# Modulation vectors of the first sub-layer: eight fp32 matmuls in one run, a small fold matmul, and a later place for the second scale and the squares

## The chip, the core and the metric

The kernel runs on one core of a Trainium2 chip. The metric is the time of one execution on the device in microseconds (us); less is better. Five engines work side by side, each through its own list of instructions: TensorE (PE in the profile, PEld for its weight loads), VectorE (DVE), ScalarE (ACT), GpSimd (POOL) and SyncE (SP), which here issues nearly all transfers.

## The reference

Two layers over 512 latent tokens and 256 context tokens, width 1024. Each sub-layer normalizes its input, scales and shifts it by vectors that come from the conditioning, and adds a gated result. Cut to what matters here:

```python
silu_c = jax.nn.silu(c)
silu_cc = jax.nn.silu(c_ctx)
for i in range(DEPTH):
    m_lat = (silu_c @ ada_w[i] + ada_b[i]).reshape(b, N_SUBLAYERS, N_MOD, 1, d)
    m_ctx = (silu_cc @ ada_w[i] + ada_b[i]).reshape(N_SUBLAYERS, N_MOD, 1, d)
    h = norm_modulate(x_lat, norm_g[i, 0], m_lat[:, 0, 0], m_lat[:, 0, 1])   # rms_norm(x, g) * (1 + scale) + shift
    x_lat = x_lat + MACARON_WEIGHT * m_lat[:, 0, 2] * swiglu(h, ffn_w_in[i, 0], ffn_w_out[i, 0])
    ...
```

The first sub-layer (a SwiGLU feed-forward) needs three such vectors of 1024 numbers, shift, scale and gate, each for the latent and for the context conditioning. They are the subject of the change.

## The kernel before

Everything is kept with features on the 128 partitions and tokens along the free dimension. A product in nearly full fp32 precision is made of three fp32r matmuls (`mm3`, L882 to L885): high part of the weights by high part of the data, high by low, low by high. ScalarE makes a high part by a copy (L206), VectorE the low part by a subtraction (L207). Input products of a feed-forward are done by Strassen-like products of half-size blocks; the first three output chunks of the first sub-layer go straight instead, so that they can begin before the norm is known.

Those straight products are twelve numbered steps. Steps 0 to 2 are the chunks 0 to 2 with the first half of K and the first 384 tokens ("00"), steps 3 to 5 the same chunks with the second half of K ("01"), steps 6 to 8 and 9 to 11 the same for the second 384 tokens. A step has four rounds k of six matmuls (gate and up weights, three each), 24 in all; step 0 uses the tile tB11 (the scaled input, high and low), step 3 tB21, step 6 tB12. The table `hooks` (L1804 to L1821) says what else is written behind round k of step n: the entry (3, 1) is emitted behind round 1 of step 3. While these steps last, TensorE, SyncE, ScalarE and VectorE all run in the written order, so the table fixes what stands ahead of what in each queue.

A modulation vector is computed as two half vectors hm of 512 numbers: hm 2 and 3 are the scale, 0 and 1 the shift, 4 and 5 the gate. In the hooks they are called scale0, scale1, shift0, shift1, gate0 and gate1. One half vector goes through `ada_direct` (L496) in stages, each `run(..., 1)` doing one:

1. Four fp32 matmuls (L501), k = 0 to 3. Each has 128 x 32 weights (`silu_p`, of whose 32 columns two are used) and 512 columns of `ada_w`, and goes to its own 32 columns of TensorE's array and its own 32 partitions of one PSUM bank.
2. Four more, k = 4 to 7, that add to the same places.
3. ScalarE copies the bank to SBUF (`adr`, L507).
4. Four transposes by TensorE (L511) of 128 x 128 each, VectorE's sum over the four groups (`ads`, L513), and VectorE's addition of the bias into `mods` (L484).

The second scale half also needs `scale_vec` (L669, the tile `scl`); then "early" (L800 to L808) makes tB21 of the input and that scale, ScalarE the high and VectorE the low part. "fill" splits the weights of a following step (w or lateG tiles). "squares" has ScalarE square an input chunk (L628) and VectorE add it to `ssq` (L633); "parts" splits the sum (th by ScalarE, L652; tl by VectorE, L653); "root" has TensorE add it over the partitions by two matmuls with ones (L663, L664) and ScalarE and VectorE form the inverse root from it (y, r; L641 to L645). "root_sum" and "root_rest" are the two halves of the same for the second 384 tokens.

Of the kernel before, what the change touches and what calls it, by code (L numbers as in the profile page):

```python
# [10 lines left out]
F32 = mybir.dt.float32  # L11
# [123 lines left out]
def backbone(ctx: ExitStack, tc: tile.TileContext, a: dict, out: bass.AP):  # L135
    nc = tc.nc
    act, dve, pe = nc.scalar, nc.vector, nc.tensor
# [358 lines left out]
    def ada_direct(i, hm, loaded, tag, turned="S"):  # L496

        ps = ptile(tag)
        for k in range(KC):
            g = 32 * (k % 4)  # L500
            pe.matmul(ps[g : g + 32, :], boot_tiles["silu"][:, k, :], loaded[k](), start=(k < 4), stop=(k >= 4), tile_position=(0, g), skip_group_check=True)  # L501
            if hm in boot_raws:
                raw_used(boot_raws[hm][k // 2])
            if k % 4 == 3:
                yield
        row = tmp.tile([P, NL], F32, name=f"adr{hm}", tag="t")
        act.activation(row, ps, AF.Copy)  # L507
        yield
        pt = ptile(turned, (P, 4, P))
        for j in range(4):  # L510
            pe.transpose(pt[:, j, :], row[:, j * P : (j + 1) * P], boot_tiles["ident"])  # L511
        sums = boot_tiles["sums"]
        dve.tensor_reduce(out=sums, in_=pt.rearrange("p j (g c) -> p j c g", g=4)[:, :, :2, :], axis=AX.X, op=ALU.add)  # L513
        ada_put(i, hm, sums, range(2))
        ada_done.add((i, hm))
        yield

# [1205 lines left out]
    with tc.tile_pool(name="apool", bufs=1) as apool, tc.tile_pool(name="g0", bufs=1) as gp, tc.tile_pool(name="qp", bufs=1) as qp, psum(A=3, B=1, C=3, S=1):  # L1723
# [24 lines left out]
        with tc.tile_pool(name="boot", bufs=1) as bp, aw_pool():  # L1748
            in_order()
            op = opening(0, 0)  # L1750
            ada_setup(bp)
            preload_ln_exp()
            raw_homes[5] = lambda: gp.tile([P, D], F32, name="raw5", tag="G0")
            late = {}

            def late_tile(tag, q):
                if tag not in late:
                    late[tag] = gp.tile([P, 3, D // 2], F32R, name=f"late{tag}", tag=tag)
                return late[tag][:, q, :]
# [24 lines left out]
            keep_busy(4)  # L1784
            w_fill(1)
            run(scale0, 2)
            keep_busy(5)
            scale_vec(0, 0, slice(0, 4))
            w_fill(1)
            op["early"](0)  # L1790

            def do(*items):
                def go():
                    for name, *args in items:
                        own[name](*args) if name in own else op[name](*args)
                return go

            def scale_put():
                run(scale1, 1)
                scale_vec(0, 0, slice(4, 8))  # L1800

            own = {"scale1": lambda n: run(scale1, n), "shift0": lambda n: run(shift0, n), "shift1": lambda n: run(shift1, n),
                   "gate0": lambda n: run(gate0, n), "gate1": lambda n: run(gate1, n), "fill": w_fill, "raws": raw_fill, "put": scale_put}
            hooks = {(0, 0): do(("fill", 2)), (0, 1): do(("squares", 0, range(4))), (0, 2): do(("fill", 2)), (0, 3): do(("scale1", 1)),  # L1804
                     (1, 0): do(("squares", 0, range(4, 8)), ("fill", 2)), (1, 1): do(("scale1", 1)), (1, 2): do(("scale1", 1)), (1, 3): do(("put",)),
                     (2, 0): do(("early", 1)), (2, 1): do(("parts", 0)), (2, 2): do(("fill", 2)), (2, 3): do(("fill", 2)),
                     (3, 0): do(("root", 0)), (3, 1): do(("squares", 1, range(KC))), (3, 3): do(("parts", 1)),
                     (4, 1): do(("shift0", 1)), (4, 2): do(("shift0", 1)), (4, 3): do(("shift0", 1), ("evict",), ("root_sum", 1), ("shift0", 1), ("root_rest", 1)),
                     (5, 0): do(("normed", 0, 1, 0), ("modulated", 0, 1, 0, "short"), ("normed", 0, 1, 1), ("parted", 0, 1, 0, "hi", 2), ("shift_columns", 0), ("parted", 0, 1, 0, "lo")),
                     (5, 1): do(("shift1", 1)), (5, 2): do(("shift1", 1)),  # L1810
                     (5, 3): do(("shift1", 1), ("modulated", 0, 1, 1, "short"), ("normed", 1, 1, 0), ("parted", 0, 1, 1), ("normed", 1, 1, 1)),
                     (6, 0): do(("shift1", 1), ("evict",), ("modulated", 1, 1, 0), ("parted", 1, 1, 0, "both", 2), ("shift_columns", 1)),
                     (6, 1): do(("modulated", 1, 1, 1), ("normed", 0, 0, 0), ("parted", 1, 1, 1)),
                     (6, 2): do(("gate0", 1), ("modulated", 0, 0, 0), ("normed", 0, 0, 1), ("parted", 0, 0, 0)), (6, 3): do(("gate0", 1)),
                     (7, 0): do(("gate0", 1), ("raws",), ("modulated", 0, 0, 1), ("normed", 1, 0, 0), ("parted", 0, 0, 1)),
                     (7, 1): do(("modulated", 1, 0, 0), ("normed", 1, 0, 1), ("sums", "T1", 0), ("parted", 1, 0, 0)),
                     (7, 3): do(("gate0", 1), ("modulated", 1, 0, 1), ("sums", "T1", 1), ("parted", 1, 0, 1)),
                     (8, 0): do(("sum_parted", "T1", 0), ("sum_parted", "T1", 1), ("sums", "T2", 0), ("sums", "T2", 1)), (8, 2): do(("gate1", 1)), (8, 3): do(("gate1", 1)), (9, 0): do(("gate1", 1), ("raws",)), (9, 1): do(("gate1", 1)),
                     (11, 0): do(("fill", 2)), (11, 2): do(("fill", 2)),
                     (14, "out", 2): do(("sums", "T3", 0, True), ("sums", "T3", 1, True)), (14, "out", 3): do(("sum_parted", "T2", 0, True), ("sum_parted", "T2", 1, True)),  # L1820
                     14: do(("sums", "T4", 0), ("sums", "T4", 1), ("sum_parted", "T3", 0), ("sum_parted", "T3", 1), ("sum_parted", "T4", 0), ("sum_parted", "T4", 1))}  # L1821
            op1 = opening(0, 1)
            ffn(gp, 0, 0, op1, TOKENS, hooks, op)
# [93 lines left out]
```

## Time and profile before

| what | value |
|---|---|
| median of 3 runs | 2396.28 us (2395.4 to 2396.76) |
| profiled execution | 2396.33 us, of which the span is 2394.0 us |
| granted TensorE clock, mean | 0.999 |
| busy: TensorE, VectorE, ScalarE, GpSimd | 2372.9, 2031.4, 1168.2, 135.4 us |
| TensorE busy in 0 to 110 us | 103.58 us |
| first fp32 matmul of a modulation vector | at 4.44 us |
| first product of the first sub-layer | at 14.62 us |

The timeline gives the start of an instruction (or of several alike that follow each other) in us from the span's start, the time to its end in us, engine, line and operation, output and inputs, and in square brackets the idle time of the engine ahead of it with what ended it. Matmuls overlap, so starts say more than durations. Other views are grouped by line: the count, then min/median/max of the duration in ns.

### The profile page before, as it was taken

What the parts mean: (1) busy time and instruction counts of PE and PEld (TensorE: products, weight loads), DVE (VectorE), ACT (ScalarE), POOL (GpSimd) and SP (SyncE); (2) the same over time, 40 slices, a digit from 0 to 9 for tenths busy, and PEclk for the clock granted to TensorE, in tenths of its full rate; (3) what the DMA queues carried; (4) which work ended last, traced back from release to release, by engine and by line L of the source; (5) the groups of instructions that cost most, each with busy time, mean ns of one, the idle gap of its engine ahead of it and who ended that gap; (6) DMA issues with size and microseconds to landing.
All of it is one profiled execution on the core that took longest, in us unless ns stands there. A gap on an engine that the chain in (4) does not pass through costs nothing.

```text
span 2394.0 us, 37639 instructions
## 1 busy us (share of the span) xinstructions
PE 2372.9 (99%) x14303; PEld 2247.7 (94%) x14303; DVE 2031.4 (85%) x4018; ACT 1168.2 (49%) x2198; POOL 135.4 (6%) x256
## 2 busy tenths in 40 slices
PE   9999999999999999999999999999999999999998
PEld 6999999999999999999999999999998889899998
DVE  6989989978988888888887988888778987988887
ACT  5634334355535653433435543343355776555555
POOL 0001101100000001000000001101100000000000
PEclk9999999999999999999999999999999999999999
DMA  9234444430334123423432144444441101133331
GB/s 338 86 112 138 130 128 129 131 115 27 106 106 133 37 66 115 127 93 119 128 103 70 49 128 124 150 137 121 140 132 45 53 10 58 67 110 102 106 107 62
DMA packets 93062, 253.71 MB, mean 106 GB/s; under 512 B 10320, under 2 KB 18640, under 8 KB 92880
## 3 DMA queue, kind: packets, MB, share of 16 engines
q1 hardware_dynamic: 71984, 183.65, 23.8%
q0 software_dynamic: 20352, 67.12, 9.5%
q8 instruction: 112, 1.84, 0.3%
q14 instruction: 70, 0.57, 0.1%
q10 hardware_dynamic: 544, 0.52, 0.1%
HBM read 249.16 MB, written 2.10 MB: 105 GB/s over the span
## 4 chain that ended last, share of the span: by engine, by line
PE 90%; DVE 4%; ACT 3%; DMA 1%; issue 1%; SPq 0%; DVEq 0%; ACTq 0%
PE ps_A L883 16%; PE ps_A L884 16%; PE ps_A L885 16%; PE ps_C L883 11%; PE ps_C L884 11%; PE ps_C L885 11%; PE ps_B L885 3%; PE ps_B L883 3%; PE ps_B L884 3%; PE ps_T L1564 1%; DMA ada<-in_ada_w 0%; DVE f L785 0%; DVE w L207 0%; DMA raw<-in_ffn_w_in 0%; ACT pr L1547 0%
## 5 line engine op out<-in xcount | busy, mean ns | idle before, releaser
L206 ACT ACTIVATE w<-raw 128x512 fp32r<-128x512 f32 (+1 forms) x862 | 523.6, 621 | 708.9 <-PE ps_A L885 219.1
L207 DVE TENSOR_TENSOR w<-raw,w 128x512 fp32r<-128x512 f32 (+1 forms) x862 | 574.6, 680 | 118.0 <-ACT w L206 104.8
L526 POOL DMA_DIRECT2D aw<-in_ada_t x240 | 129.4, 539 | 1367.0 <-DVE mods L547 1078.5
L390 DVE TENSOR_TENSOR raw<-raw,raw 128x512 f32<-128x512 f32 x264 | 181.7, 690 | 9.0 <-DMA raw<-in_ffn_w_in 4.9
L884 PE MATMUL ps_C<-gl,w 128*128 128x512 f32 (+1 forms) x548 | 188.3, 344 | 0.0
L883 PE MATMUL ps_C<-gh,w 128*128 128x512 f32 (+1 forms) x548 | 188.1, 343 | 0.0
L885 PE MATMUL ps_C<-gh,w 128*128 128x512 f32 (+1 forms) x548 | 188.0, 343 | 0.0
L883 PE MATMUL ps_A<-gh,w 128*128 128x512 f32 (+1 forms) x540 | 185.5, 343 | 0.6 <-DVE x L951 0.6
L884 PE MATMUL ps_A<-gl,w 128*128 128x512 f32 (+1 forms) x540 | 185.6, 344 | 0.0
L885 PE MATMUL ps_A<-gh,w 128*128 128x512 f32 (+1 forms) x540 | 185.4, 343 | 0.0
L547 DVE CUSTOM_DVE_ANT_0 ps_S<-aw,silu_row,packed 128x512 f32<-128x512 f32 x208 | 157.1, 756 | 2.3 <-DMA aw<-in_ada_t 0.9
L547 DVE CUSTOM_DVE_ANT_0 ps_S<-aw,silu_row,mods 128x512 f32<-128x512 f32 x208 | 157.1, 755 | 1.0
L951 DVE SCALAR_TENSOR_TENSOR x<-ps_C,gat,x 128x512 f32<-128x512 f32 (+1 forms) x158 | 99.8, 633 | 43.8 <-PE ps_C L885 43.3
L883 PE MATMUL ps_A<-tB11h,w 128*128 128x384 f32 (+1 forms) x400 | 129.6, 324 | 0.2 <-ACT tB11h L807 0.2
L884 PE MATMUL ps_A<-tB11l,w 128*128 128x384 f32 (+1 forms) x400 | 129.1, 323 | 0.2 <-DVE tB11l L808 0.2
L885 PE MATMUL ps_A<-tB11h,w 128*128 128x384 f32 (+1 forms) x400 | 128.8, 322 | 0.0
L883 PE MATMUL ps_C<-tB22h,w 128*128 128x384 f32 (+2 forms) x376 | 121.3, 322 | 0.0
L885 PE MATMUL ps_C<-tB22h,w 128*128 128x384 f32 (+2 forms) x376 | 121.2, 322 | 0.0
L884 PE MATMUL ps_C<-tB22l,w 128*128 128x384 f32 (+2 forms) x376 | 121.2, 322 | 0.0
L951 DVE SCALAR_TENSOR_TENSOR x<-ps_A,gat,x 128x512 f32<-128x512 f32 (+1 forms) x162 | 102.1, 639 | 16.5 <-PE ps_A L885 16.3
L883 PEld LDWEIGHTS ps_A<-gh,w 128*128 128x128 f32 x540 | 102.3, 189 | 14.0 <-issue 1.0
L885 PEld LDWEIGHTS ps_C<-gh,w 128*128 128x128 f32 x548 | 103.8, 189 | 12.3
(486 smaller groups left out, 6931.9 us busy)
## 6 DMA issues: line engine op xcount, KB each, us to landing
raw<-in_ffn_w_in SPq DMA_DIRECT2D x170, 512.0 KB, 3.8
aw<-in_ada_t POOLq DMA_DIRECT2D x240, 256.0 KB, 3.0
raw<-in_ffn_w_out SPq DMA_DIRECT2D x80, 512.0 KB, 4.1
raw<-in_conv_w_in SPq DMA_DIRECT2D x24, 512.0 KB, 3.7
ada<-in_ada_w SPq DMA_DIRECT2D x28, 256.0 KB, 5.3
raw<-in_attn_w_qkv SPq DMA_DIRECT2D x12, 512.0 KB, 4.5
raw<-in_ada_w SPq DMA_DIRECT2D x8, 512.0 KB, 6.3
silu_row<-in_crow POOLq DMA_DIRECT2D x8, 512.0 KB, 4.1
```

The source lines that it names most:

```text
L206: hi = act.activation(dsth, src, AF.Copy)
L207: lo = dve.tensor_tensor(out=dstl, in0=src, in1=dsth.bitcast(F32), op=ALU.subtract)
L390: dve.tensor_tensor(out=quad(o), in0=quad(x), in1=quad(y), op=ALU.subtract)
L526: nc.gpsimd.dma_start(w, a["ada_t"][t, kh, j])
L547: ins = dve.tensor_tensor_reduce(out=junk, in0=w, in1=silu_row[kh][:, v, :], scale=1.0, scalar=total if kh else ada_b[:, i, hm // 2, col : ...
L883: pe.matmul(ps, wh, xh, start=first, stop=False, **kw)
L884: pe.matmul(ps, wh, xl, start=False, stop=False, **kw)
L885: pe.matmul(ps, wl, xh, start=False, stop=last, **kw)
L951: dve.scalar_tensor_tensor(out=x, in0=p[:, o - off : o - off + w], scalar=gat[:, m, v : v + 1], in1=x, op0=ALU.mult, op1=ALU.add)
L1564: pe.transpose(pt[:, c, :], pr[:, (c0 + c) * P : (c0 + c + 1) * P], ident)
```

## The change

For five of the six half vectors (all but scale0) the eight matmuls stand in one run: the stage ends only behind k = 7. The hooks that held the first four are dropped, and scale1's whole run moves to the place behind round 1 of step 1.

In place of the four transposes and VectorE's reduce, four fp32 matmuls with the copied bank as weights and a tile `fold` of 128 x 2 as moving data turn the vector and sum its four groups at once; `fold` holds a one where the partition belongs to column c of a group, and is made once from the identity by a reduce at the start. VectorE's addition of the bias now reads PSUM.

Scale1's fold is written behind round 3 of step 1 as before, and "early" and the weight fill for step 3 follow at once. The squares 4 to 7 move from behind round 0 of step 1 to behind round 1 of step 2, "parts" from (2, 1) to (2, 3), the root from (3, 0) to (3, 1), and the fills of the weights for steps 3 to 5 from (1, 0), (2, 2) and (2, 3) to (1, 3), (2, 2) and (3, 0).

```diff
+        fold = boot_tiles["fold"] = bp.tile([P, 2], F32, name="fold", tag="fold")
+        dve.tensor_reduce(out=fold, in_=ident.rearrange("p (g c) -> p c g", g=4)[:, :2, :], axis=AX.X, op=ALU.add)
...
-            if k % 4 == 3:
+            if k == KC - 1 or (k % 4 == 3 and hm == 2):
                 yield
...
-        pt = ptile(turned, (P, 4, P))
+        pt = ptile(turned, (P, 4, 2))
         for j in range(4):
-            pe.transpose(pt[:, j, :], row[:, j * P : (j + 1) * P], boot_tiles["ident"])
-        sums = boot_tiles["sums"]
-        dve.tensor_reduce(out=sums, in_=pt.rearrange("p j (g c) -> p j c g", g=4)[:, :, :2, :], axis=AX.X, op=ALU.add)
-        ada_put(i, hm, sums, range(2))
+            pe.matmul(pt[:, j, :], row[:, j * P : (j + 1) * P], boot_tiles["fold"], start=True, stop=True, skip_group_check=True)
+        ada_put(i, hm, pt, range(2))
...
-            hooks = {(0, 0): do(("fill", 2)), (0, 1): do(("squares", 0, range(4))), (0, 2): do(("fill", 2)), (0, 3): do(("scale1", 1)),
-                     (1, 0): do(("squares", 0, range(4, 8)), ("fill", 2)), (1, 1): do(("scale1", 1)), (1, 2): do(("scale1", 1)), (1, 3): do(("put",)),
-                     (2, 0): do(("early", 1)), (2, 1): do(("parts", 0)), (2, 2): do(("fill", 2)), (2, 3): do(("fill", 2)),
-                     (3, 0): do(("root", 0)), (3, 1): do(("squares", 1, range(KC))), (3, 3): do(("parts", 1)),
+            hooks = {(0, 0): do(("fill", 2)), (0, 1): do(("squares", 0, range(4))), (0, 2): do(("fill", 2)),
+                     (1, 1): do(("scale1", 2)), (1, 3): do(("put",), ("early", 1), ("fill", 2)), (2, 1): do(("squares", 0, range(4, 8))), (2, 2): do(("fill", 2)), (2, 3): do(("parts", 0)),
+                     (3, 0): do(("fill", 2)), (3, 1): do(("root", 0), ("squares", 1, range(KC))), (3, 3): do(("parts", 1)),
...
```

The first "shift0", "shift1", "gate0" and "gate1" of the other hooks are dropped from (4, 1), (5, 1), (6, 2) and (8, 2). The lines behind the changed ones move by one or two: L501 becomes L502, L511 becomes L512, L484 becomes L485, and from L516 to the table of hooks a line's number is one less (L663 becomes L662, L883 becomes L882).

TensorE's order in step 1 before, behind round 1 (ada tiles are the weights of scale1, w_282 and w_285 those of step 1):

```order
L883 MATMUL ps_C<-tB11h,w_285 128x384
L884 MATMUL ps_C<-tB11l,w_285 128x384
L885 MATMUL ps_C<-tB11h,w_285 128x384
L501 MATMUL ps_B<-ada_174,silu_p 32x512 x2
L501 MATMUL ps_B<-ada_175,silu_p 32x512 x2
L883 MATMUL ps_A<-tB11h,w_282 128x384
```

And the same place now:

```order
L884 MATMUL ps_C<-tB11h,w_285 128x384
L502 MATMUL ps_B<-ada_174,silu_p 32x512 x3
L502 MATMUL ps_B<-ada_175,silu_p 32x512 x3
L502 MATMUL ps_B<-ada_176,silu_p 32x512 x2
L882 MATMUL ps_A<-tB11h,w_282 128x384
```

All eight stand behind round 1; the four that stood behind step 0 are gone from there.

VectorE's order between the weights of step 2 and the first root, before (w_311 and w_314 are the low parts of step 2's weights, the first lateG pair that of step 3, the second that of step 4):

```order
L207 TENSOR_TENSOR w_314<-raw_171,w_314 128x512
L633 TENSOR_TENSOR ssq<-ssq,sq 128x384 x4
L207 TENSOR_TENSOR lateG_348<-raw_157,lateG_348 128x512
L207 TENSOR_TENSOR lateG_353<-raw_159,lateG_348 128x512
L513 TENSOR_REDUCE ads<-ps_S 128x8
L484 TENSOR_TENSOR mods_103<-ads,packed 128x8
L669 SCALAR_TENSOR_TENSOR scl<-mods_103,packed 128x4 x2
L808 SCALAR_TENSOR_TENSOR tB21l<-x,scl,tB21h 128x384 x4
L653 SCALAR_TENSOR_TENSOR tl<-ssq,eps_84,th 128x384
L207 TENSOR_TENSOR lateG_353<-raw_165,lateG_353 128x512
```

And now:

```order
L207 TENSOR_TENSOR w_314<-raw_172,w_314 128x512
L485 TENSOR_TENSOR mods_103<-ps_S,packed 128x8
L668 SCALAR_TENSOR_TENSOR scl<-mods_103,packed 128x4 x2
L807 SCALAR_TENSOR_TENSOR tB21l<-x,scl,tB21h 128x384 x4
L207 TENSOR_TENSOR lateG_378<-raw_158,lateG_378 128x512
L207 TENSOR_TENSOR lateG_383<-raw_160,lateG_378 128x512
L632 TENSOR_TENSOR ssq<-ssq,sq 128x384 x4
L207 TENSOR_TENSOR lateG_383<-raw_166,lateG_383 128x512
L207 TENSOR_TENSOR lateG_424<-raw_168,lateG_424 128x512
L652 SCALAR_TENSOR_TENSOR tl<-ssq,eps_84,th 128x384
```

The four sums and the step 3 weights stood ahead of the second scale and stand behind it now, and the step 4 weights, which stood behind the root's low part tl, stand ahead of it.

More of the change, by code (lines that the diff above doesn't have):

```diff
@@ L477, in ada_setup @@
         make_identity(nc, ident)
-        boot_tiles["sums"] = bp.tile([P, 4, 2], F32, name="ads", tag="ads")
+        fold = boot_tiles["fold"] = bp.tile([P, 2], F32, name="fold", tag="fold")
+        dve.tensor_reduce(out=fold, in_=ident.rearrange("p (g c) -> p c g", g=4)[:, :2, :], axis=AX.X, op=ALU.add)
     def ada_put(i, hm, src_ps, vs):
@@ L1803, in backbone @@
                    "gate0": lambda n: run(gate0, n), "gate1": lambda n: run(gate1, n), "fill": w_fill, "raws": raw_fill, "put": scale_put}
-            hooks = {(0, 0): do(("fill", 2)), (0, 1): do(("squares", 0, range(4))), (0, 2): do(("fill", 2)), (0, 3): do(("scale1", 1)),
-                     (1, 0): do(("squares", 0, range(4, 8)), ("fill", 2)), (1, 1): do(("scale1", 1)), (1, 2): do(("scale1", 1)), (1, 3): do(("put",)),
-                     (2, 0): do(("early", 1)), (2, 1): do(("parts", 0)), (2, 2): do(("fill", 2)), (2, 3): do(("fill", 2)),
-                     (3, 0): do(("root", 0)), (3, 1): do(("squares", 1, range(KC))), (3, 3): do(("parts", 1)),
-                     (4, 1): do(("shift0", 1)), (4, 2): do(("shift0", 1)), (4, 3): do(("shift0", 1), ("evict",), ("root_sum", 1), ("shift0", 1), ("root_rest", 1)),
+            hooks = {(0, 0): do(("fill", 2)), (0, 1): do(("squares", 0, range(4))), (0, 2): do(("fill", 2)),
+                     (1, 1): do(("scale1", 2)), (1, 3): do(("put",), ("early", 1), ("fill", 2)), (2, 1): do(("squares", 0, range(4, 8))), (2, 2): do(("fill", 2)), (2, 3): do(("parts", 0)),
+                     (3, 0): do(("fill", 2)), (3, 1): do(("root", 0), ("squares", 1, range(KC))), (3, 3): do(("parts", 1)),
+                     (4, 2): do(("shift0", 1)), (4, 3): do(("shift0", 1), ("evict",), ("root_sum", 1), ("shift0", 1), ("root_rest", 1)),
                      (5, 0): do(("normed", 0, 1, 0), ("modulated", 0, 1, 0, "short"), ("normed", 0, 1, 1), ("parted", 0, 1, 0, "hi", 2), ("shift_columns", 0), ("parted", 0, 1, 0, "lo")),
-                     (5, 1): do(("shift1", 1)), (5, 2): do(("shift1", 1)),
+                     (5, 2): do(("shift1", 1)),
                      (5, 3): do(("shift1", 1), ("modulated", 0, 1, 1, "short"), ("normed", 1, 1, 0), ("parted", 0, 1, 1), ("normed", 1, 1, 1)),
@@ L1813, in backbone @@
                      (6, 1): do(("modulated", 1, 1, 1), ("normed", 0, 0, 0), ("parted", 1, 1, 1)),
-                     (6, 2): do(("gate0", 1), ("modulated", 0, 0, 0), ("normed", 0, 0, 1), ("parted", 0, 0, 0)), (6, 3): do(("gate0", 1)),
+                     (6, 2): do(("modulated", 0, 0, 0), ("normed", 0, 0, 1), ("parted", 0, 0, 0)), (6, 3): do(("gate0", 1)),
                      (7, 0): do(("gate0", 1), ("raws",), ("modulated", 0, 0, 1), ("normed", 1, 0, 0), ("parted", 0, 0, 1)),
@@ L1817, in backbone @@
                      (7, 3): do(("gate0", 1), ("modulated", 1, 0, 1), ("sums", "T1", 1), ("parted", 1, 0, 1)),
-                     (8, 0): do(("sum_parted", "T1", 0), ("sum_parted", "T1", 1), ("sums", "T2", 0), ("sums", "T2", 1)), (8, 2): do(("gate1", 1)), (8, 3): do(("gate1", 1)), (9, 0): do(("gate1", 1), ("raws",)), (9, 1): do(("gate1", 1)),
+                     (8, 0): do(("sum_parted", "T1", 0), ("sum_parted", "T1", 1), ("sums", "T2", 0), ("sums", "T2", 1)), (8, 3): do(("gate1", 1)), (9, 0): do(("gate1", 1), ("raws",)), (9, 1): do(("gate1", 1)),
                      (11, 0): do(("fill", 2)), (11, 2): do(("fill", 2)),
```

## The prediction

> **What bounds the kernel now.** I read the page first, then TensorE's timeline of the first 75 us, then the other engines' timelines beside it.
>
> ```profile
> span 2394.0 us, 37639 instructions
> PE 2372.9 (99%) x14303; PEld 2247.7 (94%) x14303; DVE 2031.4 (85%) x4018; ACT 1168.2 (49%) x2198; POOL 135.4 (6%) x256
> PE 90%; DVE 4%; ACT 3%; DMA 1%; issue 1%; SPq 0%; DVEq 0%; ACTq 0%
> ```
>
> TensorE is busy for 99% of the span and carries 90% of the chain that ended last. So the end moves by what TensorE's stream gains or loses, and by what it newly waits for. Only the first 75 us are rearranged; behind them the matmul stream is the same. What it looks like around the second scale vector:
>
> ```profile
> 19.20 0.34 PE L885 MATMUL ps_C<-tB11h,w 128*128 128x384 f32 x1
> 19.46 1.39 PE L501 MATMUL ps_B<-ada,silu_p 128*32 128x512 f32 x8
> 20.78 0.44 PE L883 MATMUL ps_A<-tB11h,w 128*128 128x384 f32 x1
> ...
> 26.11 0.34 PE L885 MATMUL ps_C<-tB11h,w 128*128 128x384 f32 x1
> 27.11 0.66 PE L511 MATMUL ps_S<-identb,adr 128*128 128x128 f32 x4 [0.67 <-ACT adr L507]
> ...
> 31.77 0.33 PE L883 MATMUL ps_A<-tB21h,lateG 128*128 128x384 f32 x1
> ...
> 32.99 0.34 PE L664 MATMUL ps_S<-tl,ones_r 128*128 128x384 f32 x1
> ...
> 36.29 0.33 PE L883 MATMUL ps_A<-tB21h,lateG 128*128 128x384 f32 x1
> ```
>
> The four transposes at 27.11 wait for ScalarE's copy, which stands behind squares and weight splits. From 31.77 the second half of K is used; at 32.99 the first root's sum ends; at 36.29 the next step begins. Now the same pieces undisturbed:
>
> ```profile
> 38.20 0.34 PE L885 MATMUL ps_C<-tB21h,lateG 128*128 128x384 f32 x1
> 38.46 0.64 PE L501 MATMUL ps_B<-ada,silu_p 128*32 128x512 f32 x4
> 38.92 0.61 PE L501 MATMUL ps_B<-ada,silu_p 128*32 128x512 f32 x4
> 39.46 0.45 PE L883 MATMUL ps_A<-tB21h,lateG 128*128 128x384 f32 x1
> 39.74 0.34 PE L884 MATMUL ps_A<-tB21l,lateG 128*128 128x384 f32 x1
> ...
> 43.08 0.34 PE L664 MATMUL ps_S<-tl,ones_r 128*128 128x384 f32 x1
> 43.25 0.60 PE L511 MATMUL ps_B<-identb,adr 128*128 128x128 f32 x4
> 43.61 0.42 PE L883 MATMUL ps_A<-tB21h,w 128*128 128x384 f32 x1
> 43.87 0.34 PE L884 MATMUL ps_A<-tB21l,w 128*128 128x384 f32 x1
> ...
> 62.29 0.66 PE L511 MATMUL ps_S<-identb,adr 128*128 128x128 f32 x4 [0.31 <-ACT adr L507]
> ```
>
> An ordinary matmul follows the last one after 0.173 us (31.77 to 36.29 are 26 of them).
>
> **One run of eight.** Four fp32 matmuls are recorded as eight: two passes, four at a time, 0.46 us apart. The group takes 38.20 to 39.74, 1.54 us, where two ordinary steps take 0.35: it costs 1.19, two groups 2.38. A run of eight has one entry and one exit: 0.26 + 3 x 0.46 + 0.54 (38.92 to 39.46) + 0.28 - 0.35 = 2.11. Gain 0.27 for each of five vectors (bounds: 0, if the second four cannot follow at once, to 0.54, the entry and exit whole).
>
> **Fold in place of transposes.** The transposes cost 43.08 to 43.87, less two steps: 0.44.
>
> ```profile
> L511 PEld LDWEIGHTS ps_S<-identb,adr x16: 138/140/143, 27.1 to 71.7; 128*128 128x128 f32 x16
> 27.11 0.42 PEld L511 LDWEIGHTS ps_S<-identb,adr 128*128 128x128 f32 x4 [0.98 <-ACT adr L507]
> 27.81 0.19 DVE L513 TENSOR_REDUCE ads<-ps_S 128x8 f32<-128x32 f32 x1 [0.37 <-PE ps_S L511]
> 12.06 0.69 DVE L207 TENSOR_TENSOR w<-raw,w 128x512 fp32r<-128x512 f32 x1 [8.19 <-ACT w L206]
> ```
>
> A transpose is one pass; the fold's fp32 product should be two, as at L501, each with its own load of 128 columns. Loads follow each other after (0.42 - 0.14) / 3 = 0.093 us, the transposes after (0.60 - 0.27) / 3 = 0.11. Two moving columns hide nothing, so I take four more passes at 0.10: each fold costs 0.40 more. Bounds: 0.15 less (the 32-column loads of L501 come far closer together than these) and 0.7 more (eight loads of 0.14 laid bare, 1.12 against 0.41). I take 0.40, since the 128-column load is the nearest row. VectorE loses a reduce per vector, 0.19 and a gap of 0.03. The new reduce of the identity falls into VectorE's 8.19 us of idleness ahead of 12.06 and costs nothing; without that cover it would be some 0.2. At the start, where mods, scale and the first product hang on the first fold, this gives 0.40 - 0.22, with a shorter last pass about +0.15.
>
> **Up to the second scale's fold.** From 19.20 to 27.11 are 7.91 us. Off come 0.32 (the first group took 19.46 to 20.78, against 1.00), 0.83 (26.11 to 27.11, against 0.17) and 0.27: the squares no longer stand ahead of the copy, which can run some 1.5 us before the fold. Do the loads come in time?
>
> ```profile
> 19.81 0.14 PEld L501 LDWEIGHTS ps_B<-ada,silu_p 128*32 128x32 f32 x2 [0.19 <-DMA ada<-in_ada_w]
> 16.87 0.33 SPq L489 DMA_DIRECT2D ada<-in_ada_w  x1
> ada<-in_ada_w SPq DMA_DIRECT2D x1, 256.0 KB, 5.6
> ```
>
> The eighth, issued at 16.87, lands 5.6 us later, at 22.47. The run starts twelve matmuls after 19.37, at 21.54, and wants it at 22.46: I add 0.05. The fold then stands at 19.20 + 6.54 + 0.15 = 25.9, 1.2 us early.
>
> **Where that goes.** Squares 4 to 7, their sums and one weight fill now stand behind this scale's product on ScalarE and VectorE, and both run in written order.
>
> ```profile
> 23.68 2.55 DVE L633 TENSOR_TENSOR ssq<-ssq,sq 128x384 f32<-128x384 f32 x4 [2.60 <-ACT sq L628]
> 29.09 2.20 DVE L808 SCALAR_TENSOR_TENSOR tB21l<-x,scl,tB21h 128x384 fp32r<-128x384 f32 x4 [0.62 <-ACT tB21h L807]
> 31.21 0.61 DVE L653 SCALAR_TENSOR_TENSOR tl<-ssq,eps,th 128x384 fp32r<-128x384 f32 x1
> 31.74 1.28 DVE L207 TENSOR_TENSOR lateG<-raw,lateG 128x512 fp32r<-128x512 f32 x2
> ```
>
> Before, L808 began 1.98 us after the transposes (27.11 to 29.09), L653 stood right behind it, and its result lay ready a microsecond before 32.99. After, L808 begins 1.98 - 0.22 + 0.40 = 2.16 behind the fold, and ahead of L653 stand two weight parts, four sums, two weight parts: 2.20 + 1.28 + 2.55 + 1.28 + 0.61 = 7.92, less four overlaps of 0.08 (31.21 against 29.09 + 2.20), 7.6. So the root's second matmul can start at 25.9 + 2.16 + 7.6 = 35.65. TensorE is there earlier: 32.99 - 27.11 = 5.88, plus six matmuls (the root moved from step (3, 0) to (3, 1)) 1.04, plus 0.40, after the fold: 33.2. **A new wait of about 2.4 us**; queued behind it are the rest of step 3 and all later matmuls, and the first root. Eighteen matmuls lay between 32.99 and 36.29, now twelve: step 4 starts at 35.65 + 3.30 - 1.04 = 37.9, 1.6 late. The weights of steps 3 to 5 lie ahead of or beside this wait and cost nothing; without the wait step 3 would want its second low part (fold + 2.16 + 3.3, 31.4) at about 32: a spare of half a microsecond.
>
> **Second root and rest.**
>
> ```profile
> 33.43 0.49 ACT L641 ACTIVATE y<-ps_S 128x384 f32<-128x384 f32 x1 [0.25 <-PE ps_S L664]
> 41.39 0.62 DVE L653 SCALAR_TENSOR_TENSOR tl<-ssq,eps,th 128x384 fp32r<-128x384 f32 x1 [0.69 <-ACT th L652]
> 67.12 0.33 SPq L247 DMA_DIRECT2D raw<-in_ffn_w_in  x1
> 74.46 0.69 DVE L390 TENSOR_TENSOR raw<-raw,raw 128x512 f32<-128x512 f32 x1
> ```
>
> From the first root to the second's parts the chain takes 0.44 + 8.58 (33.43 to 42.01): 35.65 + 9.02 = 44.7. TensorE comes at 43.08 + 1.6 - 0.27 = 44.4. The first shift's gain is lost in a wait of 0.3; the delay stays 1.6. Behind it come four folds (+1.60), three merged runs (-0.81), and the wait of 0.31 at 62.29, which goes because TensorE is later by then: +2.1 in all. Later VectorE rows change places between 76 and 92 us, where TensorE had no wait: 0. SP's order is unchanged, but a raw tile issued at 67.12, when the first half of the second gate had read it, now waits for the whole run, some 3 us later; its use at 74.46 moves by 2, and it landed 4 us after issue: hidden, with 2 us to spare, and the shortfall would be the cost beyond.
>
> **The sum.** The profiled execution took 2396.33 us, 0.05 over the median of 2396.28. 2396.33 + 0.15 - 1.37 + 0.40 + 2.4 (to step 4: +1.6) + 0.5 is 2398.4. A measurement of this kernel can tell about 0.2%, 4.8 us, from no change: this is no change. With the fold's bounds through the same steps it is 2395.1 (0.15 less) to 2400.2 (0.7 more).
>
> **Rivals.** *The root does not wait* (0.14): if VectorE gets through the squares in time, the delay at step 4 is 0.15 - 1.37 + 0.40 = -0.8, and the same rest with the first shift's 0.27 gives 2395.7. Against it: 7.6 us of rows in a fixed order. *TensorE's pace drops in the new wait* (0.06):
>
> ```profile
> PEclk9999999999999999999999999999999999999999
> L501 PE MATMUL ps_C<-ada,silu_p x16: 592/991/1062, 4.4 to 11.1; 128*32 128x512 f32 x16
> L501 PE MATMUL ps_B<-ada,silu_p x40: 592/605/617, 19.5 to 46.3; 128*32 128x512 f32 x40
> ```
>
> The first run, behind 4.4 us of idleness and partly paced by its loads, took 991 ns a pass, not 605, though the page's granted clock stands at 9 in every slice. A few microseconds at 0.6 of the pace add 1.5 to 2: 2400. The wait is half as long, which speaks against it. *A plain fp32 pass is dear* (0.05), the slower side: if each fold pass follows the last only after a whole transpose's 0.27 us, a fold costs 2.2 against 0.41, 1.75 more. The first fold then adds 1.5, the chain brings step 4 to +4.3, four folds add 7, the rest takes 1.1 off: 2406.5. It decides against no change from 0.16 us a pass (0.9 a fold; 0.1 on a fold is 0.6 on the end). For it: no row shows a plain 128-column fp32 load. Against it stand the 32-column ones:
>
> ```profile
> 23.07 0.16 PEld L501 LDWEIGHTS ps_B<-ada,silu_p 128*32 128x32 f32 x8 [0.25 <-issue]
> ```
>
> Eight of them start within 0.05 us, so four that fill 128 columns need no more than about 0.03. [...]
>
> That the change does not do what it says is excluded by the instruction order.
>
> **Numbers.** Forecast 0.75, rivals as given. Faster by over 0.2% would need 4.8 us, more than all gains with free folds: 0.01. Slower by over 0.2%: the dear pass and a little more, 0.06. Same 0.93. The range takes the forecast's bounds, the first two rivals' times, and leaves out the dear pass: 2395.2 to 2400.6.
>
> **What would show it.** Right: about 96 matmul records for 48 at L502, eight for each fold at L512 some 0.1 apart; the fold of the second scale near 25.9, not waiting; VectorE without a gap from there to L652; TensorE waiting about 2.4 us at L663. Wrong: no such wait, folds of four records or of 0.2 a pass, or a wait on a DMA at the runs of eight.

## The result, and the profile after

| | before | after |
|---|---|---|
| median of 21 runs | 2396.03 us | 2400.61 us (2399.53 to 2402.59) |
| profiled execution, its span | 2396.33, 2394.0 us | 2400.44, 2398.6 us |
| ratio of the times | | 1.002, 95% interval 1.0014 to 1.0026 |

The changed kernel is 4.6 us slower; 2398.4 was predicted, with 2400.6 as the upper end. The interval of the ratio leaves out 1, so this is a change, although the prediction held that less than 4.8 us could not be told from none. The page shows almost nothing of it:

```profile
PE 2375.3 (99%) x14327; PEld 2252.7 (94%) x14327; DVE 2030.3 (85%) x4013; ACT 1165.4 (49%) x2198; POOL 134.9 (6%) x256
PEclk9999999999999999999999999999999999999999
```

TensorE is busy for 99% of the span as before, and the granted clock stands at 9 in every slice of 60 us. TensorE's timeline of the changed kernel, at the places that the prediction speaks of:

```profile
21.70 1.92 PE L502 MATMUL ps_B<-ada,silu_p 128*32 128x512 f32 x16
...
25.74 0.95 PE L512 MATMUL ps_S<-fold,adr 128*128 128x2 f32 x8
...
32.70 0.34 PE L884 MATMUL ps_C<-tB21h,lateG 128*128 128x384 f32 x1
34.34 0.45 PE L662 MATMUL ps_S<-th,ones_r 128*128 128x384 f32 x1 [1.30 <-ACT th L651]
35.48 0.45 PE L663 MATMUL ps_S<-tl,ones_r 128*128 128x384 f32 x1 [0.69 <-DVE tl L652]
35.76 0.49 PE L882 MATMUL ps_A<-tB21h,lateG 128*128 128x384 f32 x1
36.05 0.52 PE L883 MATMUL ps_A<-tB21l,lateG 128*128 128x384 f32 x1
...
39.41 0.34 PE L882 MATMUL ps_A<-tB21h,lateG 128*128 128x384 f32 x1
...
45.84 0.34 PE L663 MATMUL ps_S<-tl,ones_r 128*128 128x384 f32 x1
46.02 0.95 PE L512 MATMUL ps_B<-fold,adr 128*128 128x2 f32 x8
...
47.08 0.33 PE L883 MATMUL ps_A<-tB21l,w 128*128 128x384 f32 x1
...
97.00 0.39 PE L882 MATMUL ps_A<-gh,w 128*128 128x256 f32 x1 [1.30 <-DVE x L950]
```

Four things are to be read here. First, the merged run and the eight records of a fold are there, and the fold at 25.74 has no bracket: it no longer waits. Second, the first root waits, as forecast, until 35.48. Third, the matmuls behind it follow each other after 0.29 to 0.32 us instead of 0.173, up to 39.2. Fourth, at 97.00 TensorE waits for VectorE where before it did not. The clock of the stretch behind the root is in the windows of the changed kernel (per window: length, then busy time of PE, PEld, DVE, ACT, POOL with their counts, then the granted clock; the last two numbers are of the DMA and play no part here):

```profile
35.70:39.20 3.50, 3.50 (x12) 3.50 (x12) 2.96 (x6) 2.93 (x7) 0.00 (x0) 0.51 1.05 392
39.20:42.00 2.80, 2.80 (x17) 2.80 (x17) 2.35 (x5) 1.73 (x4) 0.00 (x0) 1.00 1.06 389
```

TensorE counts as busy in all 3.50 us of the first window, at a clock of 0.51. A busy share hides this; the clock of a short window shows it.

For the wait at 97.00, VectorE's timeline and TensorE's of the kernel before:

```profile
77.00 0.56 DVE L1264 TENSOR_TENSOR gl<-gd,gh 128x384 fp32r<-128x384 f32 x1 [0.59 <-ACT gh L1262]
...
78.51 0.96 DVE L827 TENSOR_TENSOR fT<-f,f 128x768 f32<-128x768 f32 x1 [0.49 <-PE ps_C L885]
...
91.50 0.75 DVE L951 SCALAR_TENSOR_TENSOR x<-ps_A,gat,x 128x512 f32<-128x512 f32 x1
92.30 0.39 PE L883 MATMUL ps_A<-gh,w 128*128 128x256 f32 x1
```

And VectorE's of the changed kernel:

```profile
81.64 0.96 DVE L826 TENSOR_TENSOR fT<-f,f 128x768 f32<-128x768 f32 x1 [2.15 <-PE ps_C L884]
82.52 0.55 DVE L1263 TENSOR_TENSOR gl<-gd,gh 128x384 fp32r<-128x384 f32 x1
...
96.21 0.74 DVE L950 SCALAR_TENSOR_TENSOR x<-ps_A,gat,x 128x512 f32<-128x512 f32 x1
```

The subtraction fT (it makes T4, the input of a later Strassen-like product, and goes to a tile that TensorE must have finished with) now stands ahead of a gate operation, L1263, that stood ahead of it, and VectorE waits 2.15 us for TensorE with that one queued behind. All that follows is later, also the gated addition L950 that frees the PSUM tile for 97.00. Before, that addition ended at 91.50 + 0.75 = 92.25, and TensorE took the tile at 92.30: there was no wait, and no spare either.

| TensorE's start, us | before | predicted | after | delay |
|---|---|---|---|---|
| first product | 14.62 | 14.77 | 14.75 | +0.13 |
| second scale's fold | 27.11 | 25.9 | 25.74 | -1.37 |
| first root, second matmul | 32.99 | 35.65 | 35.48 | +2.49 |
| step 4 | 36.29 | 37.9 | 39.41 | +3.12 |
| second root, second matmul | 43.08 | 44.7 | 45.84 | +2.76 |
| output group behind L950 | 92.30 | 94.4 | 97.00 | +4.70 |

(94.4 is 92.30 + 2.1.) The span is 4.6 longer, so nothing of weight happens behind 97.

### The profile page after: what moved, and what is told of

Read it like the earlier page. It is cut to its first block, busy times and chain, and to the rows that moved or that the text cites. A ratio compares the mean times of both kernels' runs of the same rounds, so it can differ in the third digit from the quotient of the medians.

```text
span 2398.6 us, 37678 instructions
## 1 busy us (share of the span) xinstructions
PE 2375.3 (99%) x14327; PEld 2252.7 (94%) x14327; DVE 2030.3 (85%) x4013; ACT 1165.4 (49%) x2198; POOL 134.9 (6%) x256
## 4 chain that ended last, share of the span: by engine, by line
PE 90%; DVE 4%; ACT 3%; DMA 1%; issue 1%; SPq 0%; DVEq 0%; ACTq 0%
PE ps_A L882 16%; PE ps_A L883 16%; PE ps_A L884 16%; PE ps_C L882 11%; PE ps_C L883 11%; PE ps_C L884 11%; PE ps_B L884 3%; PE ps_B L882 3%; PE ps_B L883 3%; PE ps_T L1563 1%; DVE w L207 1%; DMA ada<-in_ada_w 0%; ACT w L206 0%; DVE f L784 0%; DMA raw<-in_ffn_w_in 0%
## 5 line engine op out<-in xcount | busy, mean ns | idle before, releaser
L883 PE MATMUL ps_C<-gl,w 128*128 128x512 f32 (+1 forms) x548 | 188.3, 344 | 0.0
L882 PE MATMUL ps_C<-gh,w 128*128 128x512 f32 (+1 forms) x548 | 188.1, 343 | 0.0
L882 PE MATMUL ps_A<-gh,w 128*128 128x512 f32 (+1 forms) x540 | 185.5, 343 | 1.9 <-DVE x L950 1.9
L883 PE MATMUL ps_A<-gl,w 128*128 128x512 f32 (+1 forms) x540 | 185.6, 344 | 0.0
L950 DVE SCALAR_TENSOR_TENSOR x<-ps_C,gat,x 128x512 f32<-128x512 f32 (+1 forms) x158 | 99.4, 630 | 43.6 <-PE ps_C L884 43.0
L882 PE MATMUL ps_A<-tB11h,w 128*128 128x384 f32 (+1 forms) x400 | 129.4, 324 | 0.0
L883 PE MATMUL ps_A<-tB11l,w 128*128 128x384 f32 (+1 forms) x400 | 129.1, 323 | 0.2 <-DVE tB11l L807 0.2
L882 PE MATMUL ps_C<-tB22h,w 128*128 128x384 f32 (+2 forms) x376 | 121.3, 322 | 0.0
L883 PE MATMUL ps_C<-tB22l,w 128*128 128x384 f32 (+2 forms) x376 | 121.2, 322 | 0.0
L882 PEld LDWEIGHTS ps_A<-gh,w 128*128 128x128 f32 x540 | 102.3, 189 | 15.4 <-DVE x L950 1.5
L950 DVE SCALAR_TENSOR_TENSOR x<-ps_A,gat,x 128x512 f32<-128x512 f32 (+1 forms) x162 | 101.7, 637 | 16.5 <-PE ps_A L884 16.4
```

Source lines behind the costliest of these rows:

```text
L882: pe.matmul(ps, wh, xh, start=first, stop=False, **kw)
L883: pe.matmul(ps, wh, xl, start=False, stop=False, **kw)
L950: dve.scalar_tensor_tensor(out=x, in0=p[:, o - off : o - off + w], scalar=gat[:, m, v : v + 1], in1=x, op0=ALU.mult, op1=ALU.add)
```

## The experiments

The theory: beside what was predicted, the new wait is followed by 3.4 us at half the clock (some 1.5 us at step 4), and the fold changes VectorE's order, which costs the wait at 97.00 (some 1.3). Two rivals: the folds are dearer than priced, or the delay at step 4 feeds both. Each kernel has 11 runs, beside 27 to 33 runs of the kernel before on the same chip.

| kernel | median, us | against before, us | ratio, 95% interval |
|---|---|---|---|
| e2_busy | 2399.34 | +3.83 | 1.0006 to 1.0024 |
| e5_pin | 2398.80 | +3.29 | 1.0003 to 1.002 |
| e10_busy_pin | 2398.28 | +2.64 | 1.0002 to 1.002 |
| e6_fold_alone | 2399.29 | +3.78 | 1.0007 to 1.0025 |
| e9_gate_transposes | 2398.27 | +2.63 | 1.0002 to 1.002 |
| e4_transposes | 2397.88 | +2.10 | 1.0002 to 1.002 |
| e1_squares_early | 2398.30 | +2.52 | 1.0002 to 1.002 |
| e3_parts_first | 2400.64 | +4.86 | 1.0011 to 1.0029 |
| e8_runs_squares | 2394.71 | -0.80 | 0.9988 to 1.0005 |
| e7_runs_alone | 2394.94 | -0.84 | 0.9988 to 1.0006 |
| e11_squares_pin | 2395.27 | -0.37 | 0.999 to 1.0007 |

The intervals are some 4 us wide, so a difference of one microsecond between two medians is carried by the rows of the traces, not by the medians alone. A trace is of one execution: the first product stands anywhere from 14.44 us (e8_runs_squares) to 15.75 (e4_transposes), so distances within a trace say more than places.

### e2_busy: TensorE kept at work in the new wait

```diff
-                      (3, 0): do(("fill", 2)), (3, 1): do(("root", 0), ("squares", 1, range(KC))), (3, 3): do(("parts", 1)),
+                      (3, 0): do(("fill", 2)), (3, 1): do(("busy", 12), ("root", 0), ("squares", 1, range(KC))), (3, 3): do(("parts", 1)),
```

"busy" writes twelve matmuls of ones, whose result nothing uses, ahead of the first root.

> The changed kernel with twelve dummy matmuls of 512 columns on TensorE ahead of the first root, in the place where it waits from 32.9 to 35.5 us (they feed nothing). Theory (the wait itself makes TensorE slow for 3.3 us behind it): the dummies fill the wait, the matmuls behind the root start 0.17 us apart instead of 0.32, step 4 begins near 37.8 instead of 39.4, and the time falls by 1.1 to 1.6 us to about 2399.2. Rival (the slow stretch comes from what else runs there, squares and weight splits, and not from the wait): starts stay 0.32 apart, 2400.6 or more.

TensorE's timeline:

```profile
25.57 0.95 PE L512 MATMUL ps_S<-fold,adr 128*128 128x2 f32 x8
...
32.70 2.91 PE L1780 MATMUL ps_S<-ones_r 128*128 128x512 f32 x12
...
36.01 0.34 PE L663 MATMUL ps_S<-tl,ones_r 128*128 128x384 f32 x1
36.18 0.34 PE L882 MATMUL ps_A<-tB21h,lateG 128*128 128x384 f32 x1
36.36 0.35 PE L883 MATMUL ps_A<-tB21l,lateG 128*128 128x384 f32 x1
...
38.29 0.33 PE L882 MATMUL ps_A<-tB21h,lateG 128*128 128x384 f32 x1
```

And its clock behind the root:

```profile
35.70:39.20 3.50, 3.44 (x20) 3.47 (x21) 2.37 (x6) 2.68 (x6) 0.00 (x0) 1.00 1.04 378
```

The matmuls behind the root start 0.17 to 0.19 apart again, at a clock of 1.00. Squares and weight splits still run beside them, so these do not bring the slow stretch: by these two traces the idleness does (a clock of 0.51 behind 1.30 + 0.69 us of it in the changed kernel, 1.00 here), though not every time (e9_gate_transposes, below, and the last two sections). The dummies hold the root up themselves (36.01 - 25.57 = 10.44 behind the fold, against 9.74), and still step 4 (at 38.29) stands 12.72 behind the fold instead of 13.67. Of these 0.95 us the time shows 0.75, less than the 1.1 to 1.6 that were expected: the second root now waits 0.21, and the output group still 0.98 for L950.

### e5_pin and e10_busy_pin: the subtraction out of the way

```diff
-                minus(full["T4"], full[1, 0], full[0, 0], p)
+                minus(full["T4"], full[1, 0], full[0, 0], p, True)
```

This keeps T4's subtraction in the order in which it is written. That is not its place of before, as the expectations say, but some 30 us later, at 112.29 in e5_pin: it is taken out of the stretch ahead of L950.

> The changed kernel with VectorE's two subtractions for T4 (fT, L826) held in written order, so that they no longer stand ahead of the low parts and gates of the direct chunks. Theory (in the changed kernel the first T4 subtraction blocks VectorE for 2.15 us until TensorE has left step 10, the bank of the first output group is emptied late, and TensorE waits 1.3 us at 97.0): that wait goes, 1.4 us less, 2399.2. Rival (VectorE is late there only because all is late; TensorE would wait anyway): the wait stays, 2400.6.

> The changed kernel with both single remedies together: twelve dummy matmuls in front of the first root, and the subtraction of T4 kept where it stood in the list. Theory (the two causes are separate and add): the dummy matmuls alone left +3.8, the pinned subtraction took 1.3 off the changed kernel, so +2.3 to +2.7, the granted clock at 1.00 behind the root and no wait for L950 at the first output group. Rival (both remedies feed the same later chain, so that one swallows the other): +3.2 to +3.8.

In neither is there a wait for L950 at the first output group, and in e10_busy_pin the clock behind the root is 1.00. By the medians, the pin alone takes 1.29 us off (4.58 to 3.29), the dummies alone 0.75, both together 1.94 (4.58 to 2.64); the sum of the two is 2.04. Within the scatter they add, as two separate causes would, and what stays, +2.6, is near the +2.1 that was forecast.

### e6_fold_alone and e9_gate_transposes: whether the order hangs on the fold

e6_fold_alone is the kernel before with the folds in place of the transposes and nothing else. e9_gate_transposes is the changed kernel with transposes for the two gate vectors alone:

```diff
+        boot_tiles["sums"] = bp.tile([P, 4, 2], F32, name="ads", tag="ads")
...
+        if hm in (4, 5):
+            pt = ptile(turned, (P, 4, P))
+            for j in range(4):
+                pe.transpose(pt[:, j, :], row[:, j * P : (j + 1) * P], boot_tiles["ident"])
+            sums = boot_tiles["sums"]
+            dve.tensor_reduce(out=sums, in_=pt.rearrange("p j (g c) -> p j c g", g=4)[:, :, :2, :], axis=AX.X, op=ALU.add)
+            ada_put(i, hm, sums, range(2))
...
```

> The kernel before with the fold matmul in place of the transposes for all six half vectors, and nothing else. Theory (a fold costs 0.45 us more than the transposes, and its place on VectorE's list also brings the wait at the first output group): 0.13 + 5 x 0.45 - 0.3 + 1.4 over before, about 2399.5, each fold eight records some 0.11 apart. Rival (only the folds' own price): 2398.1. Rival (the fold pays for itself by the reduce that it saves): 2396.

> The changed kernel with the two gate half vectors folded by transposes and VectorE's reduce again, the other four by the fold; the hooks are those of the changed kernel. VectorE's list then has the subtraction of T4 behind gl and gd again, as before the change. Theory (slow stretch behind the root's wait about 1.5, folds 0.45 each dearer, changed VectorE order about 1.3): the wait for L950 in front of the first output group goes, the root's wait and the halved clock behind it stay, two folds of four behind the root cost 0.9 less, of which up to 0.6 comes back as waits for adr: +2.3 to +2.9 against before. Rival (the list order is not what the late L950 comes from, but the step that is three microseconds late): L950's wait stays and only the folds' price goes, +3.7 to +4.0.

In e6_fold_alone, where nothing has been moved by hand, TensorE's timeline has

```profile
95.94 0.39 PE L882 MATMUL ps_A<-gh,w 128*128 128x256 f32 x1 [1.95 <-DVE x L950]
```

So the late L950 comes with the fold and not with the moved hooks. In e9_gate_transposes VectorE's list has the gate operation (L1272 here) ahead of the subtraction (L835) again:

```profile
78.12 0.56 DVE L1272 TENSOR_TENSOR gl<-gd,gh 128x384 fp32r<-128x384 f32 x1 [0.59 <-ACT gh L1270]
...
79.37 0.96 DVE L835 TENSOR_TENSOR fT<-f,f 128x768 f32<-128x768 f32 x1 [0.22 <-PE ps_C L893]
```

VectorE waits 0.22 instead of 2.15, and the wait at the output group falls from 1.30 to 0.52; it was to go altogether, and where the 0.52 comes from is open. Behind the straight steps VectorE's order isn't fixed by hand, and going back to transposes and reduce for the gate vectors alone is enough to restore it. Whether the reduce or the transposes tip the planning of that order was not tried.

Another part of what was expected did not come: the halved clock. The root waits as long as in the changed kernel, and yet TensorE's timeline and its window read

```profile
34.05 0.44 PE L671 MATMUL ps_S<-th,ones_r 128*128 128x384 f32 x1 [1.30 <-ACT th L660]
35.19 0.44 PE L672 MATMUL ps_S<-tl,ones_r 128*128 128x384 f32 x1 [0.69 <-DVE tl L661]
35.47 0.34 PE L891 MATMUL ps_A<-tB21h,lateG 128*128 128x384 f32 x1
...
37.56 0.33 PE L891 MATMUL ps_A<-tB21h,lateG 128*128 128x384 f32 x1
```

```profile
35.40:38.90 3.50, 3.50 (x21) 3.50 (x21) 2.96 (x6) 2.94 (x7) 0.00 (x0) 1.00 1.04 386
```

Step 4, at 37.56, stands 12.11 us behind the fold (at 25.45), where it stood 13.67 behind it in the changed kernel. The 1.56 between them is the price of the slow stretch, read from two executions with the same waits. The eleven times point the same way: five executions, the profiled one among them, have a mean granted clock of 0.999 and took 2397.16 to 2397.76 us; six have 0.998 and took 2398.27 to 2399.24. The stretch seems to come in some executions and not in others, though rows exist for one alone. That the median, +2.63, lies in the range expected with the slow stretch is partly luck.

### e4_transposes: the new places without the fold

The changed kernel with transposes and VectorE's reduce throughout.

> The changed kernel with the transposes and the reduce back in place of the folds; runs of eight and the places of the hooks kept. Theory (a fold costs 0.45 more, and through VectorE's order 1.4 more at the first output group): the root's wait and the slow stretch stay, the wait at 97.0 goes; 3 us less than the changed kernel, about 1.3 to 1.6 over before. Rival (the folds cost nothing on the way to the end, the hooks all): no less than 4 over before.

The root waits 1.60 + 0.69, the clock behind it is 0.54 (36.6 to 40.1), and there is no wait at the first output group: +2.1, above the +1.3 to +1.6 that were expected. Later waits of 0.31 (for tB12l) and 0.64 (for adr), which the changed kernel does not have, make up part of what was not expected.

### e1_squares_early and e3_parts_first: two ways to shorten the root's wait

e1_squares_early puts squares, early product, parts and root back near their old places, with one run for the second scale:

```diff
-                      (1, 1): do(("scale1", 2)), (1, 3): do(("put",), ("early", 1), ("fill", 2)), (2, 1): do(("squares", 0, range(4, 8))), (2, 2): do(("fill", 2)), (2, 3): do(("parts", 0)),
-                      (3, 0): do(("fill", 2)), (3, 1): do(("root", 0), ("squares", 1, range(KC))), (3, 3): do(("parts", 1)),
+                      (1, 1): do(("scale1", 2), ("squares", 0, range(4, 8)), ("fill", 2)), (1, 3): do(("put",)),
+                      (2, 0): do(("early", 1)), (2, 1): do(("parts", 0)), (2, 2): do(("fill", 2)), (2, 3): do(("fill", 2)),
+                      (3, 0): do(("root", 0)), (3, 1): do(("squares", 1, range(KC))), (3, 3): do(("parts", 1)),
```

e3_parts_first only puts "parts" ahead of the step 4 weights (these take 1.28 us on VectorE ahead of tl, by the prediction's rows).

> The changed kernel, folds and runs of eight kept, with squares 4 to 7 and the fill for step 3 right behind the second scale's run, and parts, root and the other fills where they stood before. Theory (the later place of the squares alone makes the root's wait and the slow stretch behind it): no wait over 0.5 us at the first root, no start distance of 0.32 behind it, the first output group's wait stays; 2 to 2.6 us less than the changed kernel, about 2.2 over before. Rival (the folds delay the root as much): 4 to 4.6 over before, as the changed kernel.

> The changed kernel with the root's parts ahead of the step 4 weights instead of behind them. VectorE's low part then comes 1.25 us earlier and ScalarE's high part at the same time, so TensorE's wait at the first root shrinks from 2.6 to about 2.0 us. [...] Theory B (any wait of a microsecond slows it, in proportion to its length): the slow stretch shrinks with the wait to about 2.5 us. Rival (the wait costs only its length): 0.6 less than the changed kernel in any case.

In the profiled execution of e1_squares_early the root waits 0.17 and the clock stays at 1.00; the late L950 (0.99) is left. It took 2396.93 us, the fastest of its eleven, so the rows explain less than the median. In e3_parts_first the wait is shorter, and yet there is no gain; the wait for L950 is 1.61 here. Its TensorE timeline:

```profile
33.54 0.34 PE L884 MATMUL ps_C<-tB21h,lateG 128*128 128x384 f32 x1
35.19 0.44 PE L662 MATMUL ps_S<-th,ones_r 128*128 128x384 f32 x1 [1.31 <-ACT th L651]
35.84 0.44 PE L663 MATMUL ps_S<-tl,ones_r 128*128 128x384 f32 x1 [0.21 <-DVE tl L652]
36.12 0.34 PE L882 MATMUL ps_A<-tB21h,lateG 128*128 128x384 f32 x1
...
36.48 0.38 PE L884 MATMUL ps_A<-tB21h,lateG 128*128 128x384 f32 x1
36.66 0.52 PE L882 MATMUL ps_C<-tB21h,lateG 128*128 128x384 f32 x1
36.98 0.52 PE L883 MATMUL ps_C<-tB21l,lateG 128*128 128x384 f32 x1
```

The clock drops here too, behind 1.31 + 0.21 us of idleness, and only 0.8 us after TensorE is at work again (from 35.84 to 36.66).

### e7_runs_alone and e8_runs_squares: the runs of eight without the fold

e7_runs_alone is the kernel before with one run for the four shift and gate vectors. e8_runs_squares has a run for the second scale as well, with the transposes and the squares right behind that run's hook; the root stands where it stood before.

> The kernel before with one run of eight for shift and gate (four vectors) and nothing else; second scale, transposes and hooks as before. Theory (each run saves TensorE 0.27 us, but from the second root on ScalarE and VectorE set the pace until the gate's copy): 0.3 to 0.6 less than before. Rival (nothing takes it back): 1.1 less.

> Five runs of eight and the early second scale as in the changed kernel, but with the transposes, and with squares 4 to 7 and the fill for step 3 right behind the second scale's run, and parts, root and the other fills where they stood before. Theory (the run saves 0.27 us a vector, the early copy 1.15, and the squares behind the copy do not delay the root): no wait of TensorE at the fold, none over 0.3 at either root, 2.9 us less than before, 2393.1. Rival (the saving of the runs is lost in the chain from the first root to the second): 2395 to 2396.

By the medians the runs gain little: 0.84 for four, where 0.27 each makes 1.1, and about as much with the fifth; both intervals include no change. In the trace of e7_runs_alone the distance from the first product to the first output matmuls of 256 columns is 75.48 us (14.96 to 90.44), before it was 76.22 (14.62 to 90.84): 0.74 less, more than the 0.3 to 0.6 expected and less than the rival's 1.1. In e8_runs_squares TensorE is early and then waits:

```profile
32.26 0.44 PE L664 MATMUL ps_S<-tl,ones_r 128*128 128x384 f32 x1 [0.30 <-DVE tl L653]
...
61.66 0.65 PE L511 MATMUL ps_S<-identb,adr 128*128 128x128 f32 x4 [0.63 <-ACT adr L507]
```

My forecast for it was far too good: I had taken the whole lead of the second scale into the end, and ScalarE and VectorE could not follow.

### e11_squares_pin: a version without either stall

> The changed kernel with the squares, the early product, the parts and the root back near their old places behind one run for the second scale, and the subtraction of T4 kept where it stood. Theory: the hooks alone gave +2.5 with a wait of 0.99 for L950, so this takes 0.9 to 1.3 off: +1.2 to +1.6, what is left being the six folds' price less the runs' saving. Rival (the folds' price is less than their records say, and the order of VectorE's list is all that was left): 0 or below.

It came out at -0.37, below what I had expected; the number of the rival, and its reason is wrong. TensorE's timeline of e11_squares_pin:

```profile
70.84 0.95 PE L512 MATMUL ps_S<-fold,adr 128*128 128x2 f32 x8
...
90.62 0.28 PE L882 MATMUL ps_A<-gh,w 128*128 128x256 f32 x1
```

Before, these two places stood at 71.51 and 90.84: the lead shrinks from 0.67 to 0.22 across one fold, which is 0.45, the price that the records gave. What I had misjudged was the starting point, the median of e1_squares_early. In its trace, weight loads wait for data:

```profile
40.72 0.14 PEld L502 LDWEIGHTS ps_B<-ada,silu_p 128*32 128x32 f32 x2 [0.52 <-DMA ada<-in_ada_w]
```

Its first shift run, which begins at 39.10, took 2.67 us, and the same run took 1.92 in e11_squares_pin. With the 0.99 of L950 this is 1.74, and the two profiled executions are 1.78 apart (2396.93 and 2395.15). The two medians are 2.9 apart; what the slower executions of e1_squares_early lose besides, no trace shows. With both stalls away, six folds and five runs come out level with the kernel before. No version here beats it by more than can be measured.

## Why the prediction was wrong

Right, with their sizes:

- **The first product** came at 14.75, 14.77 forecast. Over the traces of this case it lies between 14.44 and 15.75, so an agreement this close is partly luck.
- **The run of eight** takes 1.92 us by its records, and its eighth load was in time: no bracket at 21.70. Step 4 to the second root shrank by 0.36 (0.27 forecast).
- **The fold** takes 46.02 to 47.08, 1.06 us to the second matmul behind it, where the transposes took 43.25 to 43.87, 0.62. It is 0.44 dearer (0.40 forecast, and 0.45 across the fold of e11_squares_pin). The loads of the changed kernel, grouped:

```profile
L512 PEld LDWEIGHTS ps_S<-fold,adr x32: 186/192/192, 25.6 to 74.8; 128*128 128x128 f32 x32
L512 PE MATMUL ps_S<-fold,adr x32: 166/251/272, 25.7 to 74.9; 128*128 128x2 f32 x32
```

A load is recorded with 192 ns, the transposes' with 140, but eight passes in 0.95 us are (0.95 - 0.25) / 7 = 0.10 apart, as the transposes are 0.11. The fold's passes follow each other no slower than the transposes; there are twice as many.

- **Up to the second scale's fold**: 25.74 against 25.9, and no wait there.
- **The new wait.** VectorE runs from the fold to tl as laid out:

```profile
26.73 0.17 DVE L485 TENSOR_TENSOR mods<-ps_S,packed 128x8 f32<-128x8 f32 x1 [5.52 <-PE ps_S L512]
...
27.78 2.21 DVE L807 SCALAR_TENSOR_TENSOR tB21l<-x,scl,tB21h 128x384 fp32r<-128x384 f32 x4 [0.61 <-ACT tB21h L806]
29.90 1.29 DVE L207 TENSOR_TENSOR lateG<-raw,lateG 128x512 fp32r<-128x512 f32 x2
31.10 2.54 DVE L632 TENSOR_TENSOR ssq<-ssq,sq 128x384 f32<-128x384 f32 x4
33.60 1.29 DVE L207 TENSOR_TENSOR lateG<-raw,lateG 128x512 fp32r<-128x512 f32 x2
34.81 0.61 DVE L652 SCALAR_TENSOR_TENSOR tl<-ssq,eps,th 128x384 fp32r<-128x384 f32 x1
```

No bracket stands between L807 and L652. The root's second matmul came at 35.48, 0.17 early. Without a wait it would have followed the matmul at 32.70 by two steps of 0.173, at 33.05: 2.4 us, as forecast. (At 32.99 before, where the prediction lets the root's sum end, its second matmul starts; the sum uses the time as a start, so nothing changes.) ScalarE's th, which the prediction left out, came late as well (1.30 of the wait), but ahead of tl.

Wrong, two steps of the sum:

- **Step 4.** The prediction had "step 4 starts at 35.65 + 3.30 - 1.04 = 37.9": twelve matmuls at 0.173 behind the wait. From there to step 4 it took 39.41 - 35.48 = 3.93 us instead, at a clock of 0.51, and step 4 came 1.5 later than forecast. This was written down as a rival, with a price that fits ("add 1.5 to 2") and a chance of 0.06, because "the wait is half as long". The only row for it was a run behind 4.4 us of idleness; nothing in the trace of before showed that 2 us would be safe. In e2_busy the clock stays at 1.00 once the wait is filled, and e9_gate_transposes, where the same waits left the clock alone, has step 4 at 12.11 behind the fold, as the prediction had it (37.9 - 25.9 = 12.0).
- **The place behind the straight steps.** "Later VectorE rows change places between 76 and 92 us, where TensorE had no wait: 0." That TensorE did not wait for the old order says nothing on the new one. The row that should have been read is VectorE's addition that ends at 92.25 for a matmul at 92.30: a spare of nothing. The new order cost 1.3 (e5_pin 1.29 in time; the row at 97.00: 1.30).

A third, smaller: the second root was to wait 0.3 for tl. With step 4 this late VectorE was ahead, and the wait did not come. So 2.1 + 1.5 + 1.3 - 0.3 = 4.6, which is what was measured. Smaller still, the wait of 0.31 at 62.29 did not go altogether: the fold's first load still waits 0.32 for adr, and the fold comes at 64.78, 0.32 behind the matmul ahead of it instead of 0.173.

The rival on the dear fp32 pass fell (0.10 us a pass, where it had 0.27), and so did the root that does not wait. The late raw tile, costed at nothing, caused no wait.

## What to carry to other kernels

Where an edit puts a new wait like the ones here (1.5 to 2.3 us in all) in front of TensorE, price as a chance that the matmuls behind it run at about half the clock for a few microseconds (here 0.51 for some 3.4 us, 1.5 to 1.6 us of time; four of five traces with such a wait at the root showed it), and look at the granted clock in windows of that size, since the page's slices of 60 us average it away. When instructions change places on an engine, the wait that matters is not the one that stands in the old trace but the spare: how long before its use each result was ready. And an edit can change the order of what a scheduler places behind it, here some 50 us later; compare the orders there too and cost each row that has moved ahead of another.

## What the runs showed of the hardware

The drop of the clock did not follow the length of a wait. It came behind waits of 1.30 + 0.69 us with one matmul between (changed kernel: at half pace from about 35.8 to 39.2, 3.4 us; e5_pin, same waits: from about 36.8 to 40.2, beginning 1.1 us after TensorE had resumed), of 1.60 + 0.69 (e4_transposes), and of 1.31 + 0.21 (e3_parts_first: from 36.66 to about 40.0, beginning 0.8 us after TensorE had resumed). It did not come behind the same 1.30 + 0.69 in e9_gate_transposes, nor behind the single wait of 1.95 us in e6_fold_alone, whose window behind it reads

```profile
95.90:97.40 1.50, 1.46 (x9) 1.38 (x10) 1.50 (x4) 0.00 (x0) 0.00 (x0) 1.00 0.76 202
```

with a clock of 1.00. Without such a wait at the root no drop shows: in the trace of before the clock is 1.00 in each window of two microseconds from 14 to 110 us, in e2_busy it is 1.00 from 28 to 42, and in e1_squares_early, e8_runs_squares and e10_busy_pin no matmul of 384 columns from 15 to 110 us is recorded with more than 0.45 us, where the slow stretches have 0.52. So waits of 1.52 us in all (e3_parts_first) were followed by a drop, and waits of 1.99 us in all (e9_gate_transposes) were not. Nor was TensorE idle for most of the time ahead of it: in the 3.4 us ahead of 36.66 in e3_parts_first it was at work until 33.88, for 0.44 us from 35.19 and from 35.84 on, 1.9 us in all, more than half. What sets the drop off in one execution and not in another was not shown.
